# Two transformer blocks on one core: gate rows stored whole, late loads behind weights, FFN products of 512 columns

## The chip, the cores and the metric

One core of one Trainium2 chip. The metric is the device time of one execution in microseconds, the median over runs.

## The reference

256 tokens of width 1024 go through two blocks of two layers each, in fp32. The first block's layer is a gated delta rule with a convolution mixer, followed by a feed-forward (FFN); the second block is a conditioned transformer whose shifts, scales and gates come from a vector `c` and, for the context, from `c_ctx`:

```python
# first block, each layer l
x = x + concat([o_dn, o_sc]) @ w_out
h2 = rms_norm(x, norm2_g)
x = x + (silu(h2 @ ffn_w_gate) * (h2 @ ffn_w_up)) @ ffn_w_down
...
# second block, each layer l; N_MOD = 6 rows of 1024 for c, and for c_ctx 6 in layer 0, 2 in layer 1
ml = ada_mod(c, w_ada[l], b_ada[l], N_MOD)        # silu(c) @ w_ada + b_ada
mc = ada_mod(c_ctx, w_ada[l], b_ada[l], 2 if last else N_MOD)
hl = x * (1 + ml[1]) + ml[0]
x = layer_norm(ALPHA * x + ml[2] * mix(zl, attn_l), ln1_g[l], ln1_b[l])
x = layer_norm(ALPHA * x + ml[5] * ffn(x * (1 + ml[4]) + ml[3]), ln2_g[l], ln2_b[l])
```

The FFN of the first block has 22 x 128 = 2816 hidden channels (NF = 22 in the kernel).

## The kernel before

**Products.** fp32 accuracy comes from splitting each operand in a high part (`hi`, L155: a ScalarE cast to fp32r) and a low part (`lo`, L158: a VectorE subtraction), and from three products: wh·ah + wh·al + wl·ah. All matmuls are recorded under `mm` (L181), all transposes under `tr` (L184), VectorE's forms under L161 (`tt`), L165 (`ts`) and L170 (`stt`), ScalarE's activations under L178 (`act`).

**Weights** come in tiles of 512 KB (128 x 1024 fp32), one `wraw` (L208 to L212) each, on SyncE's DMA queue, which also issues every other load and store; five raw tiles, four high and three low ones are kept. SyncE issues in program order of the schedule: what stands ahead of a weight tile on this queue goes first, and an issue waits until its buffer is free.

**Two ways of multiplying.** In `fm` and `fm_mms` a weight tile is stationary: for each of eight 128 x 128 pieces one product of 256 columns (all tokens) with ah, one with al (both on wh), and then eight of 256 with wl: 24 matmuls and 24 weight loads per tile. In `tm` the activations are stationary and the moving operand is 512 columns of weights; the down projection of the FFN works so, with 12 products per tile.

**FFN of block 1** (in `block1`): `norm_fm` normalises x, transposes it to feature-major and splits it; then for j in 0..21 two weight tiles of `w1gu` (gate, up) are multiplied into the halves of one PSUM tile `pa`, ScalarE takes silu of the gate, VectorE multiplies by the up half into `y32`; after two j the pair is split into high and low `Y` (a 128 x 512 step at L158). Then comes `tm` with `w1dn`, 22 weight tiles per layer.

**Background work.** The shifts, scales and gates of the second block are vector work: `dot_begin` loads `crow` (c and c_ctx, 2 x 512 KB broadcast) and `bcol`, takes silu, and puts `dot_step`s on a list; each loads a tile of `w_ada` and multiplies it with `crow` on VectorE with a sum over the row (L754, one per context), 48 tiles per layer. `tick`, called after each weight tile, takes 0.8 of them per tile in block 1's FFN. Every eighth step closes one of the six modulation rows in `fmod`, a [128, 2, 48] tile. The gate rows (m = 2 and 5) are needed along the free dimension later, so they go to DRAM at once (`grow`, L763) and are read back, broadcast over the partitions, by `gate_sb` (L788). In layer 0 of the modulation (run during block 1, whose layers follow one another) there are two rows for two contexts, four stores; in layer 1 two.

**Order of the work.** A scheduler decides the order on each engine when the program is built; `issue_after(ins)` holds what is inside the block behind an instruction. Three loads that are needed late have no such hold: `more` (the table `lm`, called after the second tile of the first layer's first stage), `later` (tables `cst`, `p2`, `fg` and the context `cx`, called in block 1's layer 1) and `rowbc` (norm gains and biases broadcast over partitions, L794). The step `hbi` in `later` is a VectorE instruction on the table `p2`.

**Names.** "First transition" in what follows is the step from layer 0 to layer 1 of block 1 (at 360 to 395 us in the trace), "second transition" that from block 1 to block 2 (740 to 790 us). In both the norm of the new x runs between the last `w1dn` product and the first products of the next stage (`w1in`, and `w2qkv`).

Of the kernel before, what the change touches and what calls it, by code (L numbers as in the profile page):

```python
# [10 lines left out]
F32 = mybir.dt.float32  # L11
F32R = mybir.dt.float32r
# [14 lines left out]
P = 128  # L27
D = 1024
# [40 lines left out]
class Kern:  # L69
# [139 lines left out]
    def wraw(self, src, w=1024):  # L209
        wr = self.wp.tile([P, 1024], F32, name=self.nm("wr"), tag="wr", bufs=WB[0])  # L210
        self.nc.sync.dma_start(wr[:, :w], src)
        return wr  # L212
# [124 lines left out]
    def split1(self, oh, ol, k, x):  # L337
        self.hi(oh.k(k), x)
        self.lo(ol.k(k), x, oh.k(k))

    def fm2(self, nk=8, N=T, tag="H"):
        return FM(self, nk, N, F32R, tag), FM(self, nk, N, F32R, tag)
# [29 lines left out]

    def norm_fm(self, x, g):
        h = self.fm2()
        self.to_fm(self.blk(self.rms_tm(x)), g, None, h, 0)
        return h
# [69 lines left out]
    def block1(self, l, x, more=None, later=None):  # L446
# [132 lines left out]
        for i in range(4):  # L579
            qkv_tile(1, i)  # L580
            if i == 1 and more:
                more()
        beta, dec, kde, ebs, eg1 = self.decays(psba, pc, Y4)
# [24 lines left out]
        if later:  # L608
            later()

# [91 lines left out]

        h = self.norm_fm(x, pc("g2", 0, 8))
        y = self.fm2(NF, T, "Y")
        for j2 in range(NF // 2):
            y32 = self.u([P, 2, T])
            for i in range(2):
                j = 2 * j2 + i
                ps = self.psa([P, 2, T])
                self.fm(d["w1gu"][l, 2 * j], h, ps[:, 0])  # L710
                self.fm(d["w1gu"][l, 2 * j + 1], h, ps[:, 1])
                sg = self.u([P, T])
                self.act(sg, ps[:, 0], AF.Silu)
                self.tt(y32[:, i], sg, ps[:, 1], MUL)
            self.split(y[0], y[1], 2 * j2, y32)
            if j2 == 0:
                if l == 0:
                    self.dot_begin(0)
                self.rate = DOTS[0]
# [12 lines left out]
    def dot_begin(self, l):  # L732
# [4 lines left out]
        self.dots, self.bcol = mk([P, 2, 48], "dots"), mk([P, 48], "bcol")  # L737
        for c in range(2):
            self.nc.sync.dma_start(self.crow[:, c], self.d["crow"][c].partition_broadcast(P))
        self.nc.sync.dma_start(self.bcol, self.d["bcol"][l])  # L740
        with self.tc.issue_after(self.last_hi.ins):
# [4 lines left out]
    def dot_step(self, l, i, c, n):  # L746
# [6 lines left out]
        with self.tc.issue_after(self.last_lo.ins):  # L753
# [5 lines left out]
            self.tt(self.fmod[l][:, c, s], self.dots[:, c, s], self.bcol[:, s], ADD)  # L759
        if m in (2, 5):  # L760

            g = self.dp.tile([1, D], F32, name=self.nm("grow"), tag=f"g{l}{m}{c}")
            self.nc.sync.dma_start(g[0].rearrange("(n p) -> p n", p=P), self.fmod[l][:, c, s])  # L763
            self.grow[l, c, m] = g

# [17 lines left out]
    def gate_sb(self, l, c, m, tag="Y"):  # L783

        out = []
        for n in range(2):
            g = self.u([P, 512], tag)
            self.nc.sync.dma_start(g, self.grow[l, c, m][0, n * 512:n * 512 + 512].partition_broadcast(P))  # L788
            out.append(g)
        return out  # L790
# [425 lines left out]
    def regain(self, x, xn, gsrc, bsrc, after=True):  # L1216

        for b in range(2):
            s = slice(b * 512, b * 512 + 512)
            g = self.rowbc(gsrc, b)  # L1220
            bb = None if bsrc is None else self.rowbc(bsrc, b)
            with (self.tc.issue_after(self.last_lo.ins) if after else ExitStack()):
# [86 lines left out]
    def build(self):  # L1309
# [18 lines left out]

        self.grow, self.fmod = {}, [self.const([P, 2, 48], f"fmod{l}") for l in range(2)]
        self.block1(0, x, more)  # L1330
# [84 lines left out]
class FM:  # L1415
# [15 lines left out]
    def pr(self, k0, n, sl=slice(None)):  # L1431

        o = k0 % self.per
        return self.t(k0 // self.per)[:, o:o + n, sl]


# [132 lines left out]
```

## Time and profile before

| | |
|---|---|
| runs | 2176.67, 2182.74, 2183.46 us; median 2182.74 |
| profiled execution | 2175.73 us, its span 2173.8 us |
| mean granted clock of TensorE | 0.982 |
| busy: TensorE, its weight loads, VectorE, ScalarE, GpSimd | 96%, 85%, 75%, 46%, 3% |
| DMA, mean over the span | 152 GB/s |

A profile is one execution, here 7.0 us below the median of the runs. Busy TensorE includes pipelined matmuls whose ends are modelled. The chain that ended last is followed back from the last instruction to what released it; idle time on an engine that isn't on it costs nothing. In a timeline a bracket holds the idle time before an instruction and what ended it. The row of a helper's line mixes many operations, so the tiles' names (out<-in) tell them apart: `wr` raw, `wh` high, `wl` low weights, `pa` and `pb` PSUM, `H` and `Y` split activations, `T` work tiles.

### The profile page before, as it was taken

How to read it: one execution, taken by the hardware profiler on the slowest of the kernel's cores; microseconds unless marked ns; L12 is line 12 of the kernel's file. 1: busy time of each engine (PE TensorE's matmuls, PEld its weight loads, DVE VectorE, ACT ScalarE, POOL GpSimd, SP SyncE). 2: the span in 40 equal slices, each digit the busy share in tenths (PEclk: the TensorE clock that was granted, in tenths of full speed). 3: DMA queues.
4: the chain of work that ended last, by engine and by line, in shares of the span. 5: the costliest groups of instructions: out<-in, count | busy, mean ns of one | idle time of the engine just before them, and what ended most of it. 6: DMA issues, size and time to landing. Idle time of an engine off the chain costs nothing.

```text
span 2173.8 us, 32762 instructions
## 1 busy us (share of the span) xinstructions
PE 2076.3 (96%) x12672; PEld 1849.3 (85%) x12672; DVE 1636.6 (75%) x2795; ACT 1004.9 (46%) x1728; POOL 60.0 (3%) x92
## 2 busy tenths in 40 slices
PE   7999999799999979999999989999998999998997
PEld 7998997799899868787887978878887789988996
DVE  6756886675688659988778678666657999868765
ACT  6535443653444343566653334313323467354552
POOL 0000000000000001000000000000000100000000
PEclk9999999899999989999999999999999999999999
DMA  7325878432587842212222325455663433555563
GB/s 261 117 78 156 269 256 227 131 117 78 167 261 253 219 125 92 80 64 78 80 86 98 112 78 180 145 159 174 229 201 118 152 122 122 175 162 179 184 195 114
DMA packets 102539, 331.13 MB, mean 152 GB/s; under 512 B 17520, under 2 KB 18160, under 8 KB 102384
## 3 DMA queue, kind: packets, MB, share of 16 engines
q1 hardware_dynamic: 102384, 329.05, 48.1%
q8 instruction: 99, 1.62, 0.3%
q14 instruction: 56, 0.46, 0.1%
HBM read 327.93 MB, written 1.07 MB: 151 GB/s over the span
## 4 chain that ended last, share of the span: by engine, by line
PE 90%; DVE 4%; DMA 2%; ACT 1%; issue 1%; POOL 0%; SPq 0%; DVEq 0%; ACTq 0%; POOLq 0%
PE pa L181 80%; PE pb L181 8%; PE pb L184 3%; DMA wr<-in_w1in 1%; DVE wl L158 1%; DMA wr<-in_w2qkv 1%; ACT T L178 1%; DVE Y L170 0%; DVE A L161 0%; DVE T L170 0%; DVE bs L1003 0%; ACT wh L155 0%; DVE T L161 0%; DVE x L170 0%; POOL s L201 0%
## 5 line engine op out<-in xcount | busy, mean ns | idle before, releaser
L181 PE MATMUL pa<-H,wh 128*128 128x256 f32 (+1 forms) x5184 | 871.3, 318 | 12.5 <-ACT H L155 4.2
L155 ACT CAST wh<-wr 128x1024 fp32r<-128x1024 f32 (+1 forms) x486 | 505.3, 1040 | 765.0 <-PE pa L181 552.9
L181 PEld LDWEIGHTS pa<-H,wh 128*128 128x128 f32 x5184 | 748.5, 192 | 82.5 <-issue 10.7
L158 DVE TENSOR_TENSOR wl<-wr,wh 128x1024 fp32r<-128x1024 f32 (+1 forms) x486 | 586.6, 1208 | 290.7 <-PE pa L181 202.4
L181 PE MATMUL pa<-H,wl 128*128 128x256 f32 (+1 forms) x2592 | 453.2, 315 | 0.0
L181 PEld LDWEIGHTS pa<-H,wl 128*128 128x128 f32 x2592 | 378.4, 191 | 28.7 <-issue 0.5
L181 PE MATMUL pa<-wh,Y 128*128 128x512 f32 x976 | 310.6, 394 | 0.8 <-DVE T L161 0.8
L170 DVE SCALAR_TENSOR_TENSOR Y<-cu,p,Y 128x512 f32<-128x512 f32 (+1 forms) x480 | 272.7, 610 | 1.8 <-ACT Y L178 1.3
L181 PEld LDWEIGHTS pa<-wh,Y 128*128 128x128 f32 x976 | 183.0, 188 | 43.6 <-issue 1.6
L181 PE MATMUL pa<-wh,H 128*128 128x512 f32 x544 | 176.3, 395 | 15.7 <-ACT H L155 12.7
L181 PE MATMUL pa<-wl,Y 128*128 128x512 f32 x440 | 171.4, 394 | 0.0
L181 PEld LDWEIGHTS pa<-wh,H 128*128 128x128 f32 x544 | 102.5, 190 | 38.5 <-ACT H L155 13.6
L181 PE MATMUL pa<-wl,H 128*128 128x512 f32 x320 | 121.4, 393 | 0.0
L754 DVE SCALAR_TENSOR_TENSOR wr<-wr,crow 128x1024 f32<-128x1024 f32 x96 | 116.8, 1218 | 0.1
L201 POOL TENSOR_TENSOR s<-s,mhalf 128x1 f32<-128x1 f32 (+2 forms) x64 | 58.3, 911 | 1915.3 <-DVE s L165 1287.6
L181 PEld LDWEIGHTS pa<-wl,Y 128*128 128x128 f32 x440 | 82.6, 188 | 19.5
L170 DVE SCALAR_TENSOR_TENSOR T<-pa,p,T 128x255 f32<-128x255 f32 (+3 forms) x160 | 86.7, 550 | 1.6
L754 DVE SCALAR_TENSOR_TENSOR prod<-wr,crow 128x1024 f32<-128x1024 f32 x64 | 78.0, 1218 | 0.0
L181 PEld LDWEIGHTS pa<-wl,H 128*128 128x128 f32 x320 | 60.7, 190 | 12.6
L178 ACT ACTIVATE T<-pa,p 128x256 f32<-128x256 f32 (+1 forms) x100 | 58.6, 597 | 26.9 <-PE pa L181 26.7
L161 DVE TENSOR_TENSOR T<-T,pa 128x256 f32<-128x256 f32 (+1 forms) x96 | 45.7, 476 | 32.5 <-PE pa L181 20.7
L178 ACT ACTIVATE A<-pb 128x512 f32<-128x512 f32 (+1 forms) x76 | 41.7, 548 | 53.9 <-PE pb L181 51.2
(165 smaller groups left out, 1847.2 us busy)
## 6 DMA issues: line engine op xcount, KB each, us to landing
wr<-in_wadat SPq DMA_DIRECT2D x96, 512.0 KB, 4.5
wr<-in_w2fm SPq DMA_DIRECT2D x96, 512.0 KB, 3.4
wr<-in_w1gu SPq DMA_DIRECT2D x88, 512.0 KB, 4.4
wr<-in_w2up SPq DMA_DIRECT2D x88, 512.0 KB, 3.5
wr<-in_w1in SPq DMA_DIRECT2D x58, 512.0 KB, 4.0
wr<-in_w1dn SPq DMA_DIRECT2D x44, 512.0 KB, 4.5
wr<-in_w2dn SPq DMA_DIRECT2D x42, 512.0 KB, 3.7
wr<-in_w2qkv SPq DMA_DIRECT2D x24, 512.0 KB, 3.7
```

What stands on the lines that cost most here:

```text
L155: self.last_hi = self.nc.scalar.copy(out, x)
L158: self.last_lo = self.nc.vector.tensor_tensor(out=out, in0=x, in1=hi.bitcast(F32), op=SUB)
L161: self.nc.vector.tensor_tensor(out=out, in0=a, in1=b, op=op)
L170: self.nc.vector.scalar_tensor_tensor(out=out, in0=a, scalar=s, in1=b, op0=op0, op1=op1)
L178: return self.nc.scalar.activation(out=out, in_=x, func=f, scale=scale, **k)
L181: self.pin(self.nc.tensor.matmul(out, lhsT=lhsT, rhs=rhs, start=start, stop=stop))
L184: self.pin(self.nc.tensor.transpose(out, x, self.ident))
L201: self.nc.gpsimd.tensor_tensor(out=r, in0=a, in1=self.mhalf[:, :n], op=ALU.pow)
L754: self.nc.vector.scalar_tensor_tensor(out=w if c == n - 1 else self.prod, in0=w, scalar=1.0, in1=self.crow[:, c], op0=MUL, op1=MUL, accum_ ...
```

## The change

Three edits. (1) In block 1's FFN the high and low parts of the normalised activations stand side by side in one buffer of 512 columns (`wide2`, class `Half`); `fm_wide` multiplies wh with both at once (eight products of 512 columns) and wl with the high part alone (eight of 256). The two halves of the PSUM tile then hold two partial sums; ScalarE copies one out (`lo`), VectorE adds the other, per weight tile. (2) The gate rows: the closing step of rows 2 and 5 transposes the whole modulation tile (now 128 x 128, `fsq`, its spare columns zeroed) on TensorE, copies it by ScalarE to `rows`, and stores per context eight rows of 128 elements; both contexts are stored after the second's sum. (3) `more` (now called after the fourth tile), `later`, the loads of `dot_begin`, and the rows of `rowbc` in `regain` are issued behind the last weight load asked for until then (`last_wr`).

```diff
     def wraw(self, src, w=1024):
         wr = self.wp.tile([P, 1024], F32, name=self.nm("wr"), tag="wr", bufs=WB[0])
-        self.nc.sync.dma_start(wr[:, :w], src)
+        self.last_wr = self.nc.sync.dma_start(wr[:, :w], src)
...
+    def fm_wide(self, src, h, ps):
+        wh, wl = self.wload(src)
+        for kt in range(8):
+            self.mm(self.fl(ps), wh[:, kt * P:kt * P + P], h[2].k(kt), kt == 0, False)
+        for kt in range(8):
+            self.mm(ps[:, 0], wl[:, kt * P:kt * P + P], h[0].k(kt), False, kt == 7)
+        self.tick()
+
+    def wide2(self):
+        b = FM(self, 8, 2 * T, F32R, "H")
+        return Half(b, 0), Half(b, T), b
...
-            if i == 1 and more:
-                more()
+            if i == 3 and more:
+                with self.tc.issue_after(self.last_wr.ins):
+                    more()
...
         if later:
-            later()
+            with self.tc.issue_after(self.last_wr.ins):
+                later()
...
-        h = self.norm_fm(x, pc("g2", 0, 8))
+        h = self.norm_fm(x, pc("g2", 0, 8), True)
...
-                ps = self.psa([P, 2, T])
-                self.fm(d["w1gu"][l, 2 * j], h, ps[:, 0])
-                self.fm(d["w1gu"][l, 2 * j + 1], h, ps[:, 1])
+                lo, gu = self.u([P, 2, T]), self.u([P, 2, T])
+                for q in range(2):
+                    ps = self.psa([P, 2, T])
+                    self.fm_wide(d["w1gu"][l, 2 * j + q], h, ps)
+                    self.act(lo[:, q], ps[:, 1], AF.Copy)
+                    self.tt(gu[:, q], lo[:, q], ps[:, 0], ADD)
                 sg = self.u([P, T])
-                self.act(sg, ps[:, 0], AF.Silu)
-                self.tt(y32[:, i], sg, ps[:, 1], MUL)
+                self.act(sg, gu[:, 0], AF.Silu)
+                self.tt(y32[:, i], sg, gu[:, 1], MUL)
...
-        for c in range(2):
-            self.nc.sync.dma_start(self.crow[:, c], self.d["crow"][c].partition_broadcast(P))
-        self.nc.sync.dma_start(self.bcol, self.d["bcol"][l])
+        with self.tc.issue_after(self.last_wr.ins):
+            for c in range(2):
+                self.nc.sync.dma_start(self.crow[:, c], self.d["crow"][c].partition_broadcast(P))
+            self.nc.sync.dma_start(self.bcol, self.d["bcol"][l])
...
-        if m in (2, 5):
-
-            g = self.dp.tile([1, D], F32, name=self.nm("grow"), tag=f"g{l}{m}{c}")
-            self.nc.sync.dma_start(g[0].rearrange("(n p) -> p n", p=P), self.fmod[l][:, c, s])
-            self.grow[l, c, m] = g
+        if m in (2, 5) and c == n - 1:
+            ps = self.psb([P, P])
+            self.tr(ps, self.fsq[l])
+            rows = self.u([P, P])
+            self.act(rows, ps, AF.Copy)
+            for c in range(n):
+                g = self.dp.tile([8, P], F32, name=self.nm("grow"), tag=f"g{l}{m}{c}")
+                self.nc.sync.dma_start(g, rows[48 * c + 8 * m:48 * c + 8 * m + 8, :])
+                self.grow[l, c, m] = g
...
-            g = self.rowbc(gsrc, b)
-            bb = None if bsrc is None else self.rowbc(bsrc, b)
+            with self.tc.issue_after(self.last_wr.ins):
+                g = self.rowbc(gsrc, b)
+                bb = None if bsrc is None else self.rowbc(bsrc, b)
```

How the order moves, at three places.

SyncE's queue at the first transition, before (`w1dn` is layer 0's down projection, `w1in` the next layer's first weights):

```order
L211 DMA wr_4052<-in_w1dn 128x1024
L211 DMA wr_4167<-in_w1in 128x1024
L763 DMA grow_4022<-fmod_99 128x8x1
L211 DMA wr_4207<-in_w1in 128x1024
L211 DMA wr_4241<-in_w1in 128x1024
L763 DMA grow_4044<-fmod_99 128x8x1
L211 DMA wr_4279<-in_w1in 128x1024
L211 DMA wr_4313<-in_w1in 128x1024
```

and with the change:

```order
L211 DMA wr_3860<-in_w1dn 128x1024
L211 DMA wr_3975<-in_w1in 128x1024
L211 DMA wr_4015<-in_w1in 128x1024
L211 DMA wr_4049<-in_w1in 128x1024
L211 DMA wr_4087<-in_w1in 128x1024
L211 DMA wr_4121<-in_w1in 128x1024
L789 DMA grow_3850<-T_3848 8x128
L789 DMA grow_3852<-T_3848 8x128
```

The stores stood ahead of the second and the fourth of the next layer's first weight tiles; now five weight tiles go first, and the stores read a work tile `T` instead of `fmod`.

VectorE in the gate and up stage of layer 0, about one pair of weight tiles; before:

```order
L158 TENSOR_TENSOR wl_2544<-wr_2540,wh_2542 128x1024
L754 SCALAR_TENSOR_TENSOR prod_2257,dots_2258<-wr_2570,crow_2256 128x1024
L161 TENSOR_TENSOR T_2402<-T_2465,pa_2403 128x256
L158 TENSOR_TENSOR wl_2577<-wr_2573,wh_2575 128x1024
L754 SCALAR_TENSOR_TENSOR wr_2570,dots_2258<-wr_2570,crow_2256 128x1024
L158 TENSOR_TENSOR wl_2612<-wr_2608,wh_2610 128x1024
L161 TENSOR_TENSOR T_2402<-T_2533,pa_2468 128x256
```

and with the change:

```order
L158 TENSOR_TENSOR wl_2578<-wr_2574,wh_2576 128x1024
L775 SCALAR_TENSOR_TENSOR prod_2241,dots_2242<-wr_2596,crow_2240 128x1024
L161 TENSOR_TENSOR T_2368<-T_2481,T_2426 128x256
L161 TENSOR_TENSOR T_2488<-T_2487,pa_2489 128x256
L158 TENSOR_TENSOR wl_2614<-wr_2610,wh_2612 128x1024
L161 TENSOR_TENSOR T_2488<-T_2487,pa_2517 128x256
L775 SCALAR_TENSOR_TENSOR wr_2596,dots_2242<-wr_2596,crow_2240 128x1024
L158 TENSOR_TENSOR Y_2118<-T_2368,Y_2107 128x512
```

Each `wl` (the low part of a weight tile) is now followed by a sum of 128 x 256 from PSUM (L161 with `pa`), besides the product of gate and up (L161 without `pa`), the modulation dots (line 754 before, 775 now) staying.

VectorE where `hbi` stands; before, among the first norm's and first weights' steps of layer 0:

```order
L170 SCALAR_TENSOR_TENSOR H_108<-pb_142,p_86,H_104 128x256
L165 TENSOR_SCALAR hbi<-p_4844 128x16
L158 TENSOR_TENSOR wl_302<-wr_298,wh_300 128x1024
L158 TENSOR_TENSOR wl_336<-wr_332,wh_334 128x1024
```

and with the change:

```order
L158 TENSOR_TENSOR wl_4445<-wr_4441,wh_4443 128x1024
L170 SCALAR_TENSOR_TENSOR s_4199<-s_4195,s_4197 128x8
L170 SCALAR_TENSOR_TENSOR T_4086<-pa_4085,p_86,T_4086 128x254
L165 TENSOR_SCALAR hbi<-p_4652 128x16
L161 TENSOR_TENSOR m_7788<-fg,m_7786 128x8
L170 SCALAR_TENSOR_TENSOR s_4203<-s_4199,s_4201 128x8
L170 SCALAR_TENSOR_TENSOR T_4086<-pa_4085,p_86,T_4086 128x253
L158 TENSOR_TENSOR wl_4505<-wr_4501,wh_4503 128x1024
```

`hbi` moved to layer 1's first stage, among the convolutions (L170), ahead of `wl_4505`, and `m<-fg` with it.

## Rows read from the trace of the kernel before

**Rows 1.** The page's chain that ended last: share of the span by line.
```profile
PE pa L181 80%; PE pb L181 8%; PE pb L184 3%; DMA wr<-in_w1in 1%; DVE wl L158 1%; DMA wr<-in_w2qkv 1%; ACT T L178 1%; DVE Y L170 0%; DVE A L161 0%; DVE T L170 0%; DVE bs L1003 0%; ACT wh L155 0%; DVE T L161 0%; DVE x L170 0%; POOL s L201 0%
```

**Rows 2.** Chain in order of time, both transitions: start us, us, what.
```profile
369.61 19.71 DMA wr<-in_w1in
...
750.66 19.28 DMA wr<-in_w2qkv
...
775.38 5.21 PE pa L181 x12
780.60 0.87 PE pb L184 x8
```

**Rows 3.** DMA issues: count, KB each, median us to landing.
```profile
wr<-in_w1in SPq DMA_DIRECT2D x58, 512.0 KB, 4.0
...
grow<-fmod SPq DMA_DIRECT2D x6, 4.0 KB, 11.7
```

**Rows 4.** Timeline of SyncE, first transition: start us, us, operation, count.
```profile
365.71 0.38 SPq L763 DMA_DIRECT2D grow<-fmod  x1
...
369.61 15.43 SPq L211 DMA_DIRECT2D wr<-in_w1in  x5
```

**Rows 5.** Timeline of ScalarE, both transitions; in brackets idle before and its releaser.
```profile
389.43 1.04 ACT L155 CAST wh<-wr 128x1024 fp32r<-128x1024 f32 x1 [6.71 <-DMA wr<-in_w1in]
...
768.55 1.04 ACT L155 CAST wh<-wr 128x1024 fp32r<-128x1024 f32 x1 [7.98 <-DMA wr<-in_w2qkv]
...
770.99 2.83 ACT L178 ACTIVATE T<-pb,fmod,m 128x256 f32<-128x256 f32 x6
```

**Rows 6.** Timeline of TensorE: start, transition inside layer 0, both transitions.
```profile
15.37 5.22 PE L181 MATMUL pa<-H,wh 128*128 128x256 f32 x29 [1.09 <-ACT wh L155]
...
26.02 2.15 PE L181 MATMUL pa<-H,wh 128*128 128x256 f32 x16 [0.78 <-DVE s L170]
...
186.90 3.28 PE L184 MATMUL pb<-ident,T 128*128 128x128 f32 x16 [3.42 <-DVE T L165]
...
386.00 1.94 PE L184 MATMUL pb<-ident,T 128*128 128x128 f32 x8 [6.54 <-DVE T L165]
393.36 1.97 PE L184 MATMUL pb<-ident,T 128*128 128x128 f32 x8 [5.41 <-DVE T L165]
...
775.38 0.80 PE L181 MATMUL pa<-wh,H 128*128 128x512 f32 x1 [11.49 <-ACT H L155]
...
786.81 0.50 PE L181 MATMUL pa<-wh,H 128*128 128x512 f32 x1 [1.25 <-ACT H L155]
```

**Rows 7.** Windows: us, busy PE, PEld, DVE, ACT, POOL, clock, DMA share, GB/s.
```profile
575.00:710.00 135.00, 135.00 (x1080) 132.78 (x1080) 114.72 (x169) 63.44 (x85) 0.00 (x0) 1.00 0.77 251
775.40:780.40 5.00, 5.00 (x12) 3.94 (x13) 4.46 (x15) 2.68 (x9) 1.32 (x2) 0.53 0.01 4
787.00:790.00 3.00, 3.00 (x14) 2.46 (x14) 2.21 (x6) 2.94 (x10) 0.00 (x0) 1.00 0.00 0
```

**Rows 8.** Timeline of VectorE at the start.
```profile
20.23 0.17 DVE L165 TENSOR_SCALAR hbi<-p 128x16 f32<-128x16 f32 x1 [3.24 <-DMA p<-in_p]
```

**Rows 9.** Timeline of VectorE in layer 1's FFN, gate and up.
```profile
600.11 0.69 DVE L158 TENSOR_TENSOR Y<-T,Y 128x512 fp32r<-128x512 f32 x1
600.72 1.22 DVE L158 TENSOR_TENSOR wl<-wr,wh 128x1024 fp32r<-128x1024 f32 x1
601.85 1.22 DVE L754 SCALAR_TENSOR_TENSOR wr<-wr,crow 128x1024 f32<-128x1024 f32 x1
...
603.00 0.41 DVE L161 TENSOR_TENSOR T<-T,pa 128x256 f32<-128x256 f32 x1
603.59 1.23 DVE L158 TENSOR_TENSOR wl<-wr,wh 128x1024 fp32r<-128x1024 f32 x1 [0.18 <-PE pa L181]
```

**Rows 10.** Timeline of VectorE in the same FFN, down projection.
```profile
715.70 1.23 DVE L158 TENSOR_TENSOR wl<-wr,wh 128x1024 fp32r<-128x1024 f32 x1 [0.43 <-issue]
...
726.90 1.23 DVE L158 TENSOR_TENSOR wl<-wr,wh 128x1024 fp32r<-128x1024 f32 x1 [0.43 <-issue]
```

More of the change, by code (lines that the diff above doesn't have):

```diff
@@ L371, in rms_heads, with norm_fm @@
         return o
-    def norm_fm(self, x, g):
-        h = self.fm2()
+    def norm_fm(self, x, g, wide=False):
+        h = self.wide2() if wide else self.fm2()
         self.to_fm(self.blk(self.rms_tm(x)), g, None, h, 0)
@@ L787, in gate_sb @@
             g = self.u([P, 512], tag)
-            self.nc.sync.dma_start(g, self.grow[l, c, m][0, n * 512:n * 512 + 512].partition_broadcast(P))
+            self.nc.sync.dma_start(g, self.grow[l, c, m][4 * n:4 * n + 4].rearrange("n p -> (n p)").partition_broadcast(P))
             out.append(g)
@@ L1327, in more @@
             self.lm, self.tri, self.neg = lm[:, 0:7], lm[:, 7], lm[:, 8]
-        self.grow, self.fmod = {}, [self.const([P, 2, 48], f"fmod{l}") for l in range(2)]
+        self.fsq = [self.const([P, P], f"fmod{l}") for l in range(2)]
+        for f in self.fsq:
+            nc.gpsimd.memset(f, 0.0)
+        self.grow, self.fmod = {}, [f[:, 0:96].rearrange("p (c n) -> p c n", c=2) for f in self.fsq]
         self.block1(0, x, more)
@@ L1434, in pr, with __init__, k @@
         return self.t(k0 // self.per)[:, o:o + n, sl]
+class Half:
+    per = 1
+    def __init__(self, base, o):
+        self.b, self.o = base, o
+    def k(self, kt, sl=slice(0, T)):
+        return self.b.k(kt, slice(self.o + sl.start, self.o + sl.stop))
 @with_exitstack
```

## The prediction

> **What bounds the kernel now.** I read the page's chain of waits first, then stretches of the trace around each edit, engine by engine. The chain is TensorE for the most part: 80% of the span is its products at L181 [rows 1]. Only two kinds of gain are to be had, therefore: time in which TensorE stands still at a place that the change touches, and time that TensorE spends per product.
>
> Standing still is rare, but the change touches two of the places where it is longest. At the end of block 1's layer 0 and at its layer 1's end the chain holds a weight load of 19.71 and one of 19.28 us [rows 2], where the median 512 KB load of w_in lands in 4.0 us [rows 3]. The reader should see three views agree here. SyncE issues `grow<-fmod` stores among the first loads of the next stage (one of them, and the five loads issued behind it from 369.61 on, in [rows 4]); such a store, 4 KB, takes 11.7 us to land, almost three times as long as a load with 128 times its bytes [rows 3]. ScalarE waits 6.71 and 7.98 us for the weights behind them [rows 5], and the squares for the next norm stand in its order behind that cast. TensorE then idles 6.54 and 5.41 us at the first transition, 11.49 and 1.25 at the second [rows 6]. The transition of the same shape inside layer 0, with no store near, costs 3.42 [rows 6]. I take the scatter of 4-byte elements for the cause.
>
> **The change, part by part**
>
> *Gate rows stored whole.* Removed are six scatters; added are four PE transposes (one per layer and gate), four ScalarE copies, and six stores of eight rows of 512 B. At the first transition both stores now stand behind all five weight loads on SyncE, at the second behind four, not between them. At the first transition (layer 0 to 1) the idle 6.54 + 5.41 = 11.95 becomes the 3.42 of the undisturbed one: **-8.5 us**. Ends: 0 (the weights stay late) and -11.95 (no idle left). At the second, 11.49 + 1.25 = 12.74 becomes 3.42 again: -9.3. Its cover: what is late next is not the norm of x, since the first products after it take the context's rows, but the 16 context transposes, which all stand behind the last `w1dn` product now; I come back to it as a rival. The clock gives something back as well: the 12 products after the long idle took 5.21 us [rows 2], 434 ns each, at a granted clock of 0.53, about the lower of its two levels, 1.2 GHz; from 787 us on it is 1.00, which is 2.4 GHz [rows 7]. At 233 ns each (worked out below) they would have taken 2.80, so 2.41 was lost. After the short idle of 3.42 the 16 transposes take 3.28 [rows 6] where 8 at full rate take 0.87 [rows 2], 16 so 1.74: 1.54 lost. The difference, 0.9, is the gain: together **-10.2**, with ends 0 and -15.2 (12.74 + 2.41). The four transposes, at 0.11 each, are lost in rounding; the four copies lie on ScalarE, which has room (below). If a copy is late, so is its store, but that is read a stage later only.
>
> *Late loads behind the weights.* At the start TensorE idles 1.09 and 0.78 us [rows 6] while the constants of later stages (2 x 512 KB `crow`, 1 MB of context and others) pass ahead of the sixth weight tile. Those two are gone: **-1.9**, ends 0 and -3.2, the wait of 3.24 that VectorE has for a late parameter table, `hbi<-p` [rows 8], a weight's low half standing behind it. That step doesn't vanish: in the new order it stands, with the gain product `m<-fg`, among the convolutions of layer 1's first stage, ahead of a `wl`. Its table is ordered behind the weight load just issued, so VectorE may wait there. Between 0 and the 3.24 seen at the start I take +1.0, nearer to nothing, because weights run some tiles ahead of their use there: **+1.0**. The two rows of the last norm's gain, loaded at the start before, now stand between the last `w1dn` tile and the first `w2qkv` on SyncE, 512 KB together: at the 251 GB/s of the FFN stretch [rows 7] they can hold the weights back by 2.1 us. I take nothing for it, since that transition's first products need no norm of x and the weights have the down projection's pace of 2.8 us per tile to catch up; 2.1 is the upper end.
>
> *Products of 512 columns.* Columns are the same; only instructions fall, from 24 to 16 per weight tile, and the weight loads before them from 24 to 16 too. The stage is TensorE throughout: 135.00 of 135.00 us, clock 1.00 [rows 7]. Its pace I take from VectorE's steps, one `wl` per tile, since single matmul records can be missing: 600.72 to 603.59 is 2.87 us [rows 9], 120 ns for each of 24 products of 256 columns. For 512 columns the same pace in the down projection: four tiles of 12 products from 715.70 to 726.90 [rows 10], 233 ns. A tile becomes 8 x 0.233 + 8 x 0.120 = 2.82, that is 0.047 saved, times 88 tiles **-4.1**.
>
> By the Trainium skill, "TensorE: Matmul & The Clock Gate", section "Back-to-back issue gap", an isolated product of N columns takes N/2.4 + 2.5 ns, so a pair of 256 costs 2.6 ns more than one of 512; over 88 x 8 pairs the sum would have 1.8 there instead of 4.1 (an estimate from that formula). The rows, at 120 and 233, lie above its 109 and 216.
>
> What must hide is the work that is added beside: per weight tile one ScalarE copy and one VectorE sum of 128 x 256. ScalarE: two copies per pair of tiles at 0.47 each (six activations of that shape in 2.83 [rows 5]) and 23 pairs in the stretch are 22 us more beside 63.44 busy in 135 [rows 7]; there is room. VectorE is the narrow place: 114.72 of 135 [rows 7]. Per pair, by distances between starts [rows 9]: 2 `wl` x 1.13, 1.6 modulation dots x 1.15 (the background rate is 0.8 per tile), 3 sums x 0.41 instead of 1, half a split Y x 0.61: 5.64, and TensorE's pair is 2 x 2.82, the same. It just fits. By whole durations (1.22, 1.22, 0.41, 0.69) it is 5.97, which is 0.23 more than the present 2 x 2.87 = 5.74; over 44 pairs FFN would then lose 10.1, not gain 4.1. I take the distances, since the steps overlap like that in the trace.
>
> **Sum:** -8.5 - 10.2 - 1.9 + 1.0 - 4.1 = -23.7. Against the profiled execution's 2175.73 this is 2152.0; the median of the three runs, 2182.74, lies 7.0 above that execution, so 2159.0.
>
> **The rivals**
>
> *The wait is replaced.* With the weights in time, the second transition may end on the context: 16 transposes at 0.109 and eight activations at 0.47, 5.5 us, the latter held to the pace of four PSUM tiles. For it: their place in the new order. Against: the undisturbed transition does as much work in 3.42. Gain 4.7 there instead of 10.2: **2164.5**.
>
> *One 512 costs two 256.* Columns alone count and FFN gains nothing: **2163.1**. For it: 233 against twice 120 is 3%, read from two stages with different operands. Against: both paces are steady there [rows 9, 10]. The Trainium skill's formula above comes near this rival.
>
> *The change doesn't do what it says.* The loads at the transitions are late because the DMA engines are full with weights and modulation rows (DMA share 0.77 in FFN [rows 7]), not for the scatter. Then only 1.9 + 4.1 - 1.0 = 5.0 is left: **2177.7**, no change. Against: 4.0 us per load everywhere else.
>
> *VectorE becomes the bound of FFN* (slower). If each of the five steps `wl`, `wl` and sums waits 0.18 for its product, as the last of [rows 9] does, a pair takes 5.97 + 5 x 0.18 = 6.87, 1.13 above 5.74; 44 pairs lose 49.7, and with the other gains of 19.6 the time is **2212.8**. It decides for slower from a pair of 6.33 on, where FFN's loss passes 19.6 + 6.5 us (0.3%, about what a measurement of this kernel can tell from no change). For it: 114.72 of 135 busy before 2 sums per pair come on top. Against: tiles of weights are kept three to five deep, so that single waits average out.
>
> **How the numbers follow.** My forecast has 0.68, the replaced wait 0.10, 512 as dear as two 256 0.08, no effect at the transitions 0.07, VectorE as the bound 0.07 (0.02 of it within 0.3%). Faster is 0.68 + 0.10 + 0.08 = 0.86, within 0.3% 0.07 + 0.02 = 0.09, slower 0.05. The range: down to 2146, which is the transitions at their other ends (-3.4, -5.0), +1.0 gone, and 3 of scatter between runs; up to 2175, which holds both small rivals and FFN at 5.97 per pair (2173.2). No effect and VectorE as the bound lie outside.
>
> **What would show it.** Transitions right: TensorE's idle near the first `w1in` of layer 1 under 5 us in sum, no load of 19 us in the chain, `grow` landing in well under 11.7. Wrong if ScalarE still waits over 5 us for `w1in` or `w2qkv`. FFN right: `wl` starts 2.8 us apart, TensorE without idle; wrong from 3.0 on, with products waiting for `wl`. Start right: the `hbi` step gone from there. The forecast as a whole is wrong if the time is above 2175.

## The result, and the profile after

The changed kernel takes 2156.58 us (median of 4 runs, 2151.03 to 2157.71); the kernel before, run beside it, 2180.45. The ratio is 0.9886, 95% interval 0.9861 to 0.9912. Forecast were 2159.0 from 2182.74, which is 0.9891. The profiled execution took 2151.03, its span 2149.3, 24.5 less than before.

TensorE's timeline in the changed kernel, with the idle time ahead of an instruction in the bracket, shows the places that the prediction spoke of and some marks between them:

```profile
185.30 3.31 PE L184 MATMUL pb<-ident,T 128*128 128x128 f32 x16 [3.42 <-DVE T L165]
...
219.40 2.08 PE L181 MATMUL pa<-H,wh 128*128 128x512 f32 x8 [2.27 <-DVE T L161]
...
379.63 3.50 PE L184 MATMUL pb<-ident,T 128*128 128x128 f32 x16 [3.32 <-DVE T L165]
...
413.79 2.14 PE L181 MATMUL pa<-H,wh 128*128 128x256 f32 x16 [1.59 <-DVE T L170]
...
553.91 3.32 PE L184 MATMUL pb<-ident,T 128*128 128x128 f32 x16 [3.42 <-DVE T L165]
...
742.78 1.91 PE L184 MATMUL pb<-ident,cx 128*128 128x128 f32 x16
747.25 0.50 PE L181 MATMUL pa<-wh,H 128*128 128x512 f32 x1 [2.57 <-ACT H L155]
...
761.43 0.50 PE L181 MATMUL pa<-wh,H 128*128 128x512 f32 x1 [1.64 <-ACT H L155]
...
1156.40 0.47 PE L184 MATMUL pb<-ident,T 128*128 128x128 f32 x1 [4.38 <-ACT T L178]
```

The same marks in the kernel before, as far as [rows 6] don't have them:

```profile
426.45 2.15 PE L181 MATMUL pa<-H,wh 128*128 128x256 f32 x16 [1.60 <-DVE T L170]
...
566.57 3.69 PE L184 MATMUL pb<-ident,T 128*128 128x128 f32 x16 [3.42 <-DVE T L165]
...
760.35 0.81 PE L184 MATMUL pb<-ident,cx 128*128 128x128 f32 x6
...
1181.77 0.47 PE L184 MATMUL pb<-ident,T 128*128 128x128 f32 x1 [4.38 <-ACT T L178]
```

The idle at the first transition was 6.54 + 5.41 = 11.95 [rows 6]; one of 3.32 is left. At the second it was 11.49 + 1.25 = 12.74; 2.57 + 1.64 = 4.21 are left. New is an idle of 2.27 in layer 0's FFN, and it waits for VectorE. A stretch between two marks is the distance of their starts (an idle's start where one is named; the transposes of the context `cx` follow the last product of `w1dn`), so the whole difference can be laid out:

| stretch | before | after | difference |
|---|---|---|---|
| start to the norm of layer 0's FFN | 186.90 | 185.30 | -1.60 |
| layer 0's FFN, to the idle behind it | 192.56 | 191.01 | -1.55 |
| first transition, to the first convolution wait | 46.99 | 37.48 | -9.51 |
| layer 1 up to the norm of its FFN | 140.12 | 140.12 | 0.00 |
| layer 1's FFN, to the last product of `w1dn` | 193.78 | 188.87 | -4.91 |
| second transition, mixer of block 2 | 421.42 | 413.62 | -7.80 |
| rest, to the span's end | 992.03 | 992.90 | +0.87 |

Ten of the 16 context transposes stood among the products of layer 1's FFN before; now all 16 stand behind it. At 0.11 each, about 1.1 us has moved from the row of that FFN to the row behind it. A second profile of the changed kernel (under "The changed kernel again") has the rows from the first transition to the mixer within 1.2 us of these, but not the first two: 186.77 to the norm, and 194.23 for layer 0's FFN, which is longer than before. What the first two rows gain is within what one kernel varies from execution to execution.

At the first transition SyncE now issues five loads of w_in one after another, the stores behind them:

```profile
360.76 8.73 SPq L211 DMA_DIRECT2D wr<-in_w1in  x5
371.67 0.68 SPq L789 DMA_DIRECT2D grow<-T  x2
```

and ScalarE's casts of these weights no longer wait for a DMA, as one did for 6.71 us [rows 5], but for TensorE to give a buffer back:

```profile
374.72 1.05 ACT L155 CAST wh<-wr 128x1024 fp32r<-128x1024 f32 x1 [2.47 <-PE pa L181]
```

The chain that ended last holds no weight load at either transition any more. The prediction's third sign, stores that land in well under 11.7 us, can't be read, since the profile gives no landing time for the stores of whole rows.

In the FFN the products of 512 columns show up as groups of eight (0.23 us each), with eight of 256 between them. The starts of the groups with `wh` lie 2.79 us apart (three tiles from 205.72 to 214.09), where a tile took 2.87 before [rows 9]:

```profile
205.72 2.00 PE L181 MATMUL pa<-H,wh 128*128 128x512 f32 x8
207.56 1.12 PE L181 MATMUL pa<-H,wl 128*128 128x256 f32 x8
208.51 2.00 PE L181 MATMUL pa<-H,wh 128*128 128x512 f32 x8
...
214.09 2.09 PE L181 MATMUL pa<-H,wh 128*128 128x512 f32 x8
```

VectorE in the windows of the same run is busy 113.18 of 115 us in layer 1's FFN (114.72 of 135 before [rows 7]). The columns are those of [rows 7]; the clock is the third number from the right:

```profile
219.40:221.40 2.00, 2.00 (x9) 1.66 (x10) 2.00 (x3) 0.21 (x1) 0.00 (x0) 1.00 0.90 287
575.00:690.00 115.00, 115.00 (x647) 100.53 (x647) 113.18 (x190) 67.10 (x113) 0.00 (x0) 1.00 0.82 267
```

### The profile page after: what moved, and what is told of

It is laid out like the page before. It is cut to its first block, busy times and chain, and to the rows that moved or that the text cites. A ratio compares the mean times of both kernels' runs of the same rounds, so it can differ in the third digit from the quotient of the medians.

```text
span 2149.3 us, 31586 instructions
## 1 busy us (share of the span) xinstructions
PE 2068.3 (96%) x11972; PEld 1810.3 (84%) x11972; DVE 1661.4 (77%) x2883; ACT 1031.9 (48%) x1820; POOL 59.8 (3%) x94
## 4 chain that ended last, share of the span: by engine, by line
PE 90%; DVE 5%; issue 1%; ACT 1%; POOL 0%; DVEq 0%; ACTq 0%; POOLq 0%
PE pa L181 80%; PE pb L181 8%; PE pb L184 3%; DVE wl L158 1%; ACT T L178 1%; DVE Y L170 0%; DVE A L161 0%; DVE bs L1029 0%; DVE T L161 0%; DVE T L170 0%; DVE wr L775 0%; POOL s L201 0%; DVE x L170 0%; DVE prod L775 0%; DVE Y L167 0%
## 5 line engine op out<-in xcount | busy, mean ns | idle before, releaser
L181 PE MATMUL pa<-H,wh 128*128 128x256 f32 (+1 forms) x4480 | 861.7, 340 | 12.2 <-DVE T L170 3.2
L181 PEld LDWEIGHTS pa<-H,wh 128*128 128x128 f32 x4480 | 697.1, 191 | 105.7 <-issue 14.9
L181 PEld LDWEIGHTS pa<-H,wl 128*128 128x128 f32 x2592 | 383.5, 190 | 35.4 <-issue 0.5
L170 DVE SCALAR_TENSOR_TENSOR Y<-cu,p,Y 128x512 f32<-128x512 f32 (+1 forms) x480 | 272.6, 610 | 1.8 <-ACT Y L178 1.3
L170 DVE SCALAR_TENSOR_TENSOR T<-pa,p,T 128x255 f32<-128x255 f32 (+3 forms) x160 | 86.7, 550 | 2.4 <-ACT T L178 0.7
L161 DVE TENSOR_TENSOR T<-T,pa 128x256 f32<-128x256 f32 (+1 forms) x140 | 61.1, 455 | 24.6 <-PE pa L181 22.0
```

The costliest lines, as they stand in the source:

```text
L161: self.nc.vector.tensor_tensor(out=out, in0=a, in1=b, op=op)
L170: self.nc.vector.scalar_tensor_tensor(out=out, in0=a, scalar=s, in1=b, op0=op0, op1=op1)
L181: self.pin(self.nc.tensor.matmul(out, lhsT=lhsT, rhs=rhs, start=start, stop=stop))
```

## The experiments

**Whole rows alone.** The kernel before, with the gate rows as in the change (`fsq`, its zeroing and the reading side with them):

```diff
-            self.nc.sync.dma_start(g[0].rearrange("(n p) -> p n", p=P), self.fmod[l][:, c, s])
+            self.tr(ps, self.fsq[l])
+            self.act(rows, ps, AF.Copy)
+                self.nc.sync.dma_start(g, rows[48 * c + 8 * m:48 * c + 8 * m + 8, :])
```

> The kernel before with the gate rows stored whole and nothing else. On SyncE the stores stand behind five loads of w1in at the first transition and behind four of w2qkv at the second, as in the changed kernel. Theory (the scatter, or its place, holds the weights up): TensorE's idle at the first transition goes from 11.95 to about 3.4 us, at the second from 12.74 to about 4.2, and the time falls by 16 to 18 us. Rival (the DMA engines are full, stores don't matter): both idles stay within 2 us of before and the time doesn't move.

2163.29 us, ratio 0.9927 (0.9912 to 0.9942). TensorE at both transitions:

```profile
385.21 3.75 PE L184 MATMUL pb<-ident,T 128*128 128x128 f32 x16 [3.41 <-DVE T L165]
...
758.23 0.50 PE L181 MATMUL pa<-wh,H 128*128 128x512 f32 x1 [2.57 <-ACT H L155]
...
771.65 0.50 PE L181 MATMUL pa<-wh,H 128*128 128x512 f32 x1 [1.65 <-ACT H L155]
```

3.41 and 2.57 + 1.65: the two idles go as in the changed kernel. This part alone brings 0.73% of the 1.14%. The rival of DMA engines that are merely full falls.

**Late loads alone**, in the kernel before, run and profiled twice. Beside what stands here, `later`, the loads of `dot_begin` and the rows of `regain` are held behind `last_wr` too:

```diff
-            if i == 1 and more:
-                more()
+            if i == 3 and more:
+                with self.tc.issue_after(self.last_wr.ins):
+                    more()
```

> The kernel before with the late loads behind weights and nothing else; the scatters stay between the first weight loads at the transitions. Theory: the start is 1.6 us shorter, both transitions keep their idle of 12 us, the layer-1 stage with hbi keeps its length; the time falls by 1 to 2 us, which is no change that the median can tell. Rival (late loads share in the transitions' gain): the idle at a transition falls by over 3 us.

> The run with late loads alone once more, since its profiled execution (span 2181.2 us) lay well above the median of its runs (2175.9) and its stages can't be set beside those of before. Theory: the start is 1 to 2 us shorter, the transitions keep their idle of 12 us, time 1 to 4 us below before. Rival (more than the start is gained): some other stage is over 1.5 us shorter than in the kernel before.

2175.89 us, ratio 0.9976 (0.9963 to 0.9989), and 2171.26, ratio 0.9977 (0.9966 to 0.9987): a gain of 0.2%, about 4 us, more than the 1 to 2 us of the theory and the 1.6 us of the start. The scatters still stand between the loads here. The first profile:

```profile
387.23 1.94 PE L184 MATMUL pb<-ident,T 128*128 128x128 f32 x8 [6.58 <-DVE T L165]
395.82 1.97 PE L184 MATMUL pb<-ident,T 128*128 128x128 f32 x8 [6.65 <-DVE T L165]
...
780.11 0.79 PE L181 MATMUL pa<-wh,H 128*128 128x512 f32 x1 [12.80 <-ACT H L155]
```

and the second, of the same kernel:

```profile
384.49 1.94 PE L184 MATMUL pb<-ident,T 128*128 128x128 f32 x8 [5.73 <-DVE T L165]
389.42 1.97 PE L184 MATMUL pb<-ident,T 128*128 128x128 f32 x8 [2.99 <-DVE T L165]
...
769.13 0.79 PE L181 MATMUL pa<-wh,H 128*128 128x512 f32 x1 [9.24 <-ACT H L155]
```

6.58 + 6.65 at the first transition in one execution, 5.73 + 2.99 in the other; 12.80 and 9.24 at the second. So what the scatters cost is not a fixed amount; it moves by several us from one execution to the next, with the same order on SyncE, and by the second profile alone the rival would hold at the first transition (8.72 against 11.95), by the first it would not (13.23). Against this the other stretches of the second profile are as before: the FFN of layer 0 takes 192.57 (192.56 before), the stage with `hbi` 140.13 (140.12). Whether the late loads shorten the scatter's wait on the average, or the start alone is theirs, stays open.

**Wide products alone**, in the kernel before:

```diff
-                self.fm(d["w1gu"][l, 2 * j], h, ps[:, 0])
-                self.fm(d["w1gu"][l, 2 * j + 1], h, ps[:, 1])
+                for q in range(2):
+                    self.fm_wide(d["w1gu"][l, 2 * j + q], h, ps)
+                    self.act(lo[:, q], ps[:, 1], AF.Copy)
+                    self.tt(gu[:, q], lo[:, q], ps[:, 0], ADD)
```

> The kernel before with products of 512 columns in block 1's FFN and nothing else. Theory: weight tiles in gate and up come 2.77 to 2.82 us apart instead of 2.87, 88 of them, so 4 to 9 us less, both transitions as before. Rival 1 (columns alone count): 2.87 stays and the time with it. Rival 2 (VectorE binds): over 2.9 per tile, TensorE's products waiting for sums, time longer.

2172.18 us, ratio 0.9961 (0.9947 to 0.9975).

```profile
222.38 1.85 PE L181 MATMUL pa<-H,wh 128*128 128x512 f32 x7 [2.24 <-DVE T L161]
...
385.53 1.97 PE L184 MATMUL pb<-ident,T 128*128 128x128 f32 x8 [6.33 <-DVE T L165]
394.33 1.97 PE L184 MATMUL pb<-ident,T 128*128 128x128 f32 x8 [6.83 <-DVE T L165]
```

The stall of 2.24 in layer 0's FFN is here too, so it comes with the wide products and not with the late loads; the first transition keeps its idle, 6.33 + 6.83. At the second, where the expectation had no change, the idle is 3.13 + 3.28 + 1.95 = 8.36 instead of 12.74, although the scatters still stand among the first loads of `w2qkv` (issued at 743.70 and 746.50): once more, it varies. The three parts alone add up to 0.73 + 0.23 + 0.39 = 1.35%, the whole brings 1.14%; the intervals are wide enough for that, and the waits at the scatters, which can be saved only once, differ between all these runs.

**Scatters kept, issued later.** This and the next run cross the two things that the change does to the stores at once: their form and their place. The kernel before, with `store` called after the fourth tile of layer 1's first stage and ahead of block 2's attention:

```diff
-            self.nc.sync.dma_start(g[0].rearrange("(n p) -> p n", p=P), self.fmod[l][:, c, s])
+            self.pend.append(lambda: self.nc.sync.dma_start(g[0].rearrange("(n p) -> p n", p=P), self.fmod[l][:, c, s]))
...
+    def store(self):
+        with self.tc.issue_after(self.last_wr.ins):
+            while self.pend:
+                self.pend.pop(0)()
```

> The kernel before, with the scatters of 4-byte elements kept but issued later: at the first transition behind five loads of w1in, the place that the whole rows have in the run with whole rows alone; at the second behind the attention's loads. If the place of the store in SyncE's queue is what counts: idles of 3.4 and about 4 us as with whole rows, time 16 to 18 us less. If the scatter is slow work for the DMA engines wherever it stands: the loads issued behind it land late (10 us or more) and TensorE idles there, a few us later, so that less than half of the gain is seen.

2158.86 us, ratio 0.9902 (0.9887 to 0.9918).

```profile
382.32 1.06 PE L184 MATMUL pb<-ident,T 128*128 128x128 f32 x8 [3.39 <-DVE T L165]
...
756.71 0.50 PE L181 MATMUL pa<-wh,H 128*128 128x512 f32 x1 [1.73 <-ACT H L155]
...
765.96 0.50 PE L181 MATMUL pa<-wh,H 128*128 128x512 f32 x1 [1.26 <-ACT H L155]
```

3.39 (and 0.71 between the two halves of the transposes behind it), and 1.73 + 1.26: the long idles go, with the scatter in its old form. Most of the whole change's gain is here, with the place of six stores and nothing else, and no less than whole rows alone brought. The scatter itself is no faster. The view of DMA in 20 us around it, before, from 365 us (GB/s in 40 slices of 0.5 us; then issues, count, KB each, median us to landing in this window):

```profile
GB/s 336 320 320 336 231 79 50 50 74 57 41 41 33 33 49 57 33 33 25 33 25 33 8 74 41 262 418 345 298 363 246 83 106 57 49 66 74 107 25 33
...
wr<-in_w1in SPq DMA_DIRECT2D x7, 512.0 KB, 12.9
grow<-fmod SPq DMA_DIRECT2D x2, 4.0 KB, 15.8
```

and with the scatters behind, from 371 us:

```profile
GB/s 377 336 57 131 115 319 303 136 90 58 10 1 0 0 57 17 25 90 25 33 16 25 57 25 66 49 57 156 115 164 401 393 418 418 328 172 41 0 0 0
...
wr<-in_w1in SPq DMA_DIRECT2D x4, 512.0 KB, 9.7
grow<-fmod SPq DMA_DIRECT2D x2, 4.0 KB, 12.5
```

In both the rate falls from over 300 to under 100 GB/s for 9 to 10 us, a store takes 12.5 to 15.8 us, and the weights issued behind it take 9.7 to 12.9. In the second kernel these weights are the sixth and following, which are not needed for a while, and no wait of TensorE in that stage is longer than before.

**Whole rows, ahead of the weights.** The other half of the cross, for the first transition: the run with whole rows alone, where `gate` holds the last store for the first six loads of layer 1:

```diff
         wr = self.wp.tile([P, 1024], F32, name=self.nm("wr"), tag="wr", bufs=WB[0])
-        self.nc.sync.dma_start(wr[:, :w], src)
+        with (self.tc.issue_after(self.gate.pop(0)) if self.gate else ExitStack()):
+            self.nc.sync.dma_start(wr[:, :w], src)
```

> Whole rows alone, but at the first transition both stores are issued ahead of the first load of w1in (the loads are ordered behind them); at the second they stay where the scheduler puts them, behind four loads. If the form counts (few long pieces are quick): the idle at the first transition stays at 3 to 5 us although the stores stand ahead. If the place counts: the loads behind the stores land late again and the idle there is 8 us or more.

2161.83 us, ratio 0.9915 (0.9900 to 0.9929). TensorE, and SyncE:

```profile
383.23 3.82 PE L184 MATMUL pb<-ident,T 128*128 128x128 f32 x16 [5.50 <-DVE T L165]
...
372.47 0.68 SPq L771 DMA_DIRECT2D grow<-T  x2
373.24 24.77 SPq L212 DMA_DIRECT2D wr<-in_w1in  x11
```

The idle is 5.50, 2.1 above that of the run with the stores behind. DMA in 20 us from 371 us:

```profile
GB/s 0 0 33 0 8 8 139 147 344 328 393 442 385 377 410 418 434 410 401 442 410 434 377 295 401 320 197 246 344 238 57 0 0 0 0 0 0 0 0 0
...
wr<-in_w1in SPq DMA_DIRECT2D x8, 512.0 KB, 4.3
```

The weights behind whole rows land in 4.3 us at around 400 GB/s; there is no slow stretch behind the stores. What costs the 2.1 is that SyncE, working in order, waits for ScalarE's copy (at 372.17) and issues from 373.24 on the loads that it issues from 366.59 on in the run with whole rows alone. So form and place each do it here: short pieces must not stand ahead of weights that are needed at once, long ones may, nearly.

**Without the low sum.** The product of the high weights with the low activations is computed, and left out of the result; ScalarE's copy and VectorE's sum fall away from the changed kernel:

```diff
-                    self.act(lo[:, q], ps[:, 1], AF.Copy)
-                    self.tt(gu[:, q], lo[:, q], ps[:, 0], ADD)
+                    gus.append(ps[:, 0])
```

> The changed kernel without ScalarE's copy and VectorE's sum per weight tile in block 1's FFN (the product of the high weights with the low activations is computed and left out of the result). Theory: TensorE sets the pace, so tiles stay 2.77 to 2.80 us apart; only the one stall of 2.27 us in layer 0's FFN goes, and the time is 0 to 4 us below the changed kernel's. Rival (the sums cost time throughout): over 6 us below it.

2151.48 us, ratio 0.9871 (0.9854 to 0.9887), some 5 us below the changed kernel, between what the two theories gave; the intervals overlap, and the profiled executions don't show it (spans of 2149.7 and 2149.3). Window of layer 1's FFN:

```profile
575.00:690.00 115.00, 115.00 (x654) 100.81 (x654) 104.23 (x154) 56.58 (x74) 0.00 (x0) 1.00 0.81 271
```

VectorE has 104.23 of 115 instead of 113.18, TensorE is busy throughout in both. In the trace the stall in layer 0 is gone, and that stretch takes 189.48 instead of 191.01 (194.23 in the changed kernel's second profile).

**The sum twice**, in the changed kernel:

```diff
                     self.tt(gu[:, q], lo[:, q], ps[:, 0], ADD)
+                    self.tt(gu[:, q], lo[:, q], ps[:, 0], ADD)
```

> The changed kernel with the sum of 128 x 256 done twice per weight tile on VectorE. By distances between starts that makes 5.64 + 2 x 0.41 = 6.46 us of VectorE work per pair of tiles, above TensorE's 5.56 to 5.64. If VectorE has no slack: 0.4 to 0.9 us more per pair while dots run, 44 pairs, 18 to 40 us longer. If the modulation dots are not there for the whole stage, or steps overlap more than I reckoned: under 10 us longer.

2180.20 us, ratio 0.9998 (0.9986 to 1.0011): the change's whole gain is gone. Window of layer 1's FFN:

```profile
575.00:690.00 115.00, 105.21 (x575) 91.12 (x574) 107.48 (x189) 58.35 (x99) 0.00 (x0) 0.97 0.68 220
```

TensorE, 115.00 of 115 in the changed kernel, is down to 105.21. 2180.20 - 2156.58 = 23.6 over 44 pairs of tiles is 0.54 us per pair, within the 0.4 to 0.9 expected: of two further sums of 0.41 us per pair two thirds go to the time.

**Dots begun later**, in the changed kernel:

```diff
                 if l == 0:
                     self.dot_begin(0)
-                self.rate = DOTS[0]
+                else:
+                    self.rate = DOTS[0]
+            if j2 == 1:
+                self.rate = DOTS[0]
```

> The changed kernel with the modulation dots of layer 0's FFN begun four weight tiles later (from the second pair of pairs on), the rate unchanged. Theory: the stall of 2.27 us at 219 us comes from VectorE working off dots that had gathered while it waited for the loads and the silu of crow; begun later they don't gather, the stall goes, and the time is 1 to 3 us below the changed kernel's, too little for the median to tell but plain in the trace. Rival (it is the sum itself): the stall moves to another tile.

2156.67 us, ratio 0.9893 (0.9877 to 0.9908), like the changed kernel. The stall in layer 0 is gone, and one of the same size stands in layer 1 instead:

```profile
590.38 2.06 PE L181 MATMUL pa<-H,wh 128*128 128x512 f32 x8 [2.13 <-DVE T L161]
```

The rival holds as far as this goes: the stall is not bound to the start of the dots. Every profile here of a kernel with the sum, seven with those of the next runs, has a stall of over 2 us behind VectorE in block 1's gate and up products, and none of the seven without the sum has one there.

**The changed kernel again, the scatter in last place, and a product on GpSimd**, on one chip. The second is the changed kernel with the old scatters, issued as in the run with scatters kept; the third is the second with this beside:

```diff
-                self.tt(y32[:, i], sg, gu[:, 1], MUL)
+                self.nc.gpsimd.tensor_tensor(out=y32[:, i], in0=sg, in1=gu[:, 1], op=MUL)
```

> The changed kernel as it is, on the same chip as the next two, so that small differences can be told. Every theory: 2152 to 2160 us.

> The changed kernel with its wide products and late loads, but the gate rows scattered by 4 bytes as before and issued behind the next stage's weights (five loads of w1in at the first transition, the attention's loads at the second). If only the place behind the weights is needed: idles of 3.4 and 3 to 4 us as in the changed kernel, time within 3 us of it, or up to 4 us below, since the transposes, the copies and the wait for the copies' buffer fall away and some context transposes go back ahead of the second transition. If whole rows are needed: loads behind the scatters come late later on, TensorE idles there, and the time is 4 us or more above it.

> The run with scatters issued last, and the product of silu(gate) and up, 128 x 256, on GpSimd instead of VectorE, 44 of them. If VectorE's load in the FFN still costs time (the stall of 2.27 us and the 5 us that the run without the low sums gained): 2 to 5 us below that run. If GpSimd is slow at it (over 3 us for one) or its latency is waited for by the split of Y: no gain, or some us longer.

In this order: 2158.02 us, ratio 0.9893 (0.9874 to 0.9912); 2155.09, 0.9884 (0.9864 to 0.9904); 2152.86, 0.9876 (0.9857 to 0.9894). The whole rows are not needed where the place is right. The last has the lowest median of complete kernels, 5.2 below the changed one, but the intervals overlap; the order of the three is a hint, not shown.

GpSimd takes 1.47 us on average for a product that VectorE does in 0.41, and the traces show why little can be gained: VectorE doesn't get the time back. It is busy 114.05 of 115 us in layer 1's FFN, against 113.56 in the run beside it, and the stall in layer 0 is still there, 2.47 against 2.26. A dot beside a product on GpSimd, for instance, takes 1.77 us instead of 1.22:

```profile
601.97 1.59 POOL L736 TENSOR_TENSOR T<-T,T 128x256 f32<-128x256 f32 x1 [4.17 <-DVE T L161]
```

```profile
602.88 1.77 DVE L777 SCALAR_TENSOR_TENSOR wr<-wr,crow 128x1024 f32<-128x1024 f32 x1
```

## Why the prediction was right, and where it was wrong

The time lay 2.4 us under the forecast and within its range, and the rivals that left both transitions as they were, or made VectorE the bound, did not come about. Term by term:

*First transition, -8.5.* The idle fell by 11.95 - 3.32 = 8.6, to the 3.42 of the undisturbed transition almost exactly; the stretch is 9.5 shorter.

*Second transition, -10.2.* The stretch is 7.80 shorter. Idle fell by 12.74 - 4.21 = 8.5, not 9.3. Its first wait ends on the context, as the first rival had it: 16 transposes (1.91) and a wait of 2.57 for ScalarE, 4.47 where the rival reckoned 5.5. But the rival added this to an idle of 3.42, and it stands in its place for the most part; the second wait, 1.64, is for the rows of x and was 1.25 before. Against the forecast it costs 0.8 of idle, and about 1.1 for the ten transposes, which layer 1's FFN no longer holds. Of the 0.9 that the clock was to give back some 0.7 came: it is 0.59 from 747.20 to 751.40 and 1.00 behind that, and the 19 products up to 753.30 take 6.04 us instead of 19 x 0.230 = 4.37, so that 1.67 is lost where 2.41 was.

*FFN, -4.1.* This term is two that were both mis-sized. A tile takes 2.79 and not 2.82, which against 2.87 before is 0.08 x 88 = 7.0 gained; the eight products of 512 columns go at 0.230, not at the 0.233 of the down projection. Against it stands the stall of 2.27 in layer 0, which the sum puts at nothing: 4.8 by this reckoning. In the stretches layer 0's FFN is 1.55 shorter and layer 1's about 3.8, without the moved transposes. But where the stall is absent (dots begun later, and without the low sum) layer 0's FFN takes 188.34 and 189.48, and with it 191.01 to 194.23, so that it costs more than its 2.27. The rival by which columns alone count is out all the same, by the distance of 2.79. The Trainium skill's formula for an isolated product ("TensorE: Matmul & The Clock Gate", section "Back-to-back issue gap") would have given 1.8, an estimate; the trace does not agree, with 120 ns for 256 columns and 230 for 512, so that a pair of the former costs 10 ns more than one of the latter and not 2.5 (2.6 in the prediction). Whether the 10 ns are the product's or its weight load's is not shown: both fall from 24 to 16 per tile.

*"It just fits."* The prediction's 5.64 us of VectorE work against 5.64 of TensorE was the right reading of the load: 113.18 busy of 115. What it left out is the stall that comes with a load of this tightness, in each of the seven profiles with the sum. VectorE as the bound was only one sum per tile away, as the run with the sum twice shows. At the place of the stall VectorE works without a gap while TensorE, idle from 217.13 to 219.40, waits for the sum (`pa`), which has two dots, a product and a `wl` ahead of it:

```profile
215.08 1.22 DVE L775 SCALAR_TENSOR_TENSOR wr<-wr,crow 128x1024 f32<-128x1024 f32 x1
...
216.22 1.22 DVE L775 SCALAR_TENSOR_TENSOR prod<-wr,crow 128x1024 f32<-128x1024 f32 x1
...
217.37 0.42 DVE L161 TENSOR_TENSOR T<-T,T 128x256 f32<-128x256 f32 x1
217.71 1.22 DVE L158 TENSOR_TENSOR wl<-wr,wh 128x1024 fp32r<-128x1024 f32 x1
218.84 0.74 DVE L161 TENSOR_TENSOR T<-T,pa 128x256 f32<-128x256 f32 x2
```

*Start, -1.9, and `hbi`, +1.0.* In the profile shown the first stretch is 1.6 shorter and the waits of 1.09 and 0.78 are gone. In the second profile of the same kernel it is 0.1 shorter, with idles of 1.18, 0.78 and 0.46 at that place. Over all profiles here the first convolution's products, behind the wait at 46.86 before and 45.24 after, start at 44.79 to 47.87 without the late loads (five profiles) and at 45.21 to 46.73 with them (nine), medians 46.86 and 46.07. The ranges overlap, so that a gain of 0.8 is a guess and not shown. `hbi` costs nothing: the stage takes 140.12 in both.

*The step that failed* is a cause: "I take the scatter of 4-byte elements for the cause". It is half of it. The changed kernel stores long rows and stores them behind the weights; the prediction names the new place, but takes the form for the cause. In the run with scatters issued behind the weights the idles are 3.39 + 0.71 and 2.99 in place of 11.95 and 12.74, and the time can't be told from the changed kernel's. The stores' form matters only for what is queued right behind them and needed at once. The time came out right in spite of this because the change moved both at once, so that either cause gave the same sum. That it came within 2.4 us is luck in part: in the stretches the two transitions gave -9.5 and -7.8, the start -1.6, the FFNs -6.5, `hbi` 0 and the rest of the span +0.9, and the errors of the terms cancel.

## What to carry to other kernels

Of a transfer of few bytes in many small pieces, look at what is queued behind it: here its own landing time did not hurt, but the loads behind it took up to 12.9 us in the median instead of 4.0. Before rewriting such a store it is worth trying to issue it a few loads later; here that alone gave most of the gain.

Where an edit moves work from the bound engine to one with 85% load, count the second engine's work per step by distances between starts. If it comes out equal, expect stalls, and try the doubled work once to see how near the edge is. Moving some of the second engine's work to an idle third one may give nothing back, as the run with GpSimd shows; look at the second engine's busy time afterwards.

## What the runs showed of the hardware that was not expected

Two stores of 4 KB in pieces of 4 bytes bring the DMA rate of the core down from over 300 GB/s to between 8 and 79 for about 10 us (367.5 to 377.5 in the first view of DMA above), while the DMA engines show as busy (a share of 0.82 at 43 GB/s in these 10 us); stores of the same bytes in pieces of 512 B do not.

VectorE's steps on 128 x 1024 elements (`wl` and dots) that overlap a product on GpSimd by more than 0.3 us take 1.47 us on average, up to 1.77 (72 single ones in the two FFNs of the run with that product); the 139 others take 1.22. GpSimd's spans in a profile are rough, but the lengthening is VectorE's own.

The same stall of 2.27 us in the same kernel was followed by full speed in one execution, clock 1.00 from 219.40 to 221.40 (above), and by a slow stretch in another, eight products in 3.04 us at a granted clock of 0.63, between the two levels:

```profile
222.55 3.04 PE L181 MATMUL pa<-H,wh 128*128 128x512 f32 x8 [2.27 <-DVE T L161]
```

```profile
222.60:225.50 2.90, 2.90 (x9) 2.30 (x10) 2.90 (x5) 1.80 (x4) 0.00 (x0) 0.63 0.79 243
```

Their spans, 2149.3 and 2157.2 us, differ by more than any part of the change but the transitions, and layer 0's FFN alone by 3.2 us. A part of a few us can't be told from two medians, and from a stretch of the trace only where a second execution repeats it.
